# Short convolution of a hybrid backbone: own PSUM tile for the second sum of a pair, right-hand sums first, modulation later, output operands split block by block

## The chip, the cores and the metric

The kernel runs on one core of a Trainium2 chip. The metric is the device time of one execution in microseconds (us), as a median over runs. Before the change the three timed runs gave 1486.51, 1482.36 and 1488.16 us.

## What is computed

Four layers run one after the other over 640 tokens (512 latent, 128 context), each `x <- LayerNorm(alpha * x + gate * Mixer(x * (1 + scale) + shift))`, with shift, scale and gate from a modulation product of the condition vector. All is fp32. The change is in layer 1, the short gated convolution:

```
bg, cg, v, g = split(h @ w_in, 4)                  # h: 640 x 1024, w_in: 1024 x 4096
z = depthwise_conv3(cg * v) + conv_b
y = (silu(g) * bg * z) @ w_out                     # w_out: 1024 x 1024
```

## The kernel before, in words

**Products.** Each fp32 operand is kept as a high and a low part (`xh`, `xl` for tokens, `wh`, `wl` for weights), and a product is three matmuls: high by high, low by high, high by low. High parts are written by ScalarE (a cast), low parts by VectorE (a subtraction).

**Layer 1 (`sconv`).** The 1024 output channels of each of the four projections are cut in eight blocks j. Block 0 is computed directly: `mpair` gives cg and v, two calls of `mtile` give bg and g. For j = 1 to 7 `spair` runs twice, first for (cg, v), then for (bg, g): 14 pairs. A pair computes two 128-channel outputs over two halves of 320 tokens by a scheme with seven block products in place of eight. Each block product is 12 matmuls of 320 columns (four blocks of 128 inputs by three), 84 in a pair. In the order of the code they are

| product | weights | tokens | sum it goes to | read afterwards by |
|---|---|---|---|---|
| a | `a` | `xh` | x | ScalarE copy p1 |
| b | `b` | `xh` | y | VectorE add (p1 + y) |
| s2 | `s2` | `t2` | x | ScalarE copy u2 |
| s1 | `s1` | `t1` | z | ScalarE copy p5 |
| s3 | `s3` | `t3` | x | ScalarE copy u3 |
| s4 | `s4` | `xh` | z | VectorE add (u2 + z) |
| d | `d` | `t4` | x | ScalarE, negated |

Sums x and z go on accumulating after a copy, so the next product into the same sum has to follow the copy. Before the change x and z are the two halves of one two-bank tile `psxz` (pool `psmm`, two tiles of two banks), y is a one-bank tile `psy` (pool `psg`, four banks, which also holds the modulation's sums `psA`, the transposes `pt` and the output projection's sums `pso`).

**Operands of the pairs.** `token_sums` makes t1 to t4 once, after block 0's `mpair`: four sums and four splits of 128x1280. `_prep_pair` makes a pair's weights from one 1 MB load `praw`: casts on ScalarE, four sums and four low parts on VectorE. Pairs are numbered by their weight load, 52 to 65. Weights are double buffered.

**Modulation (`ada_unit`).** Layer 2's modulation is 12 units in layer 1, let in by a credit that grows with each weight taken (`rate` 0.45, twice that for a pair). A unit loads two 512 KB tiles `araw`, multiplies into `psA` and adds the result to `arows` on VectorE (L353).

**Output projection (`outproj`).** It first splits the mixer's output `o` into `xh`, `xl`, five token tiles of 128x1024 in turn. Then for the first 256 output columns it computes `pso` for the five token tiles (24 matmuls of 256 columns each), and VectorE folds each into the residual `z`. `z`, the affine vectors and the gate are loaded when the layer's buffers come free.

**Order.** A scheduler decides the order of instructions on each engine from its own estimates; `high_priority()` lets a block go ahead of others that are ready. An engine then executes its own list strictly in that order.

Of the kernel before, what the change touches and what calls it, by code (L numbers as in the profile page):

```python
# [9 lines left out]
F32 = mybir.dt.float32  # L10
# [3 lines left out]
ALU = mybir.AluOpType  # L14
AX = mybir.AxisListType

P = 128
D = 1024
KT = D // P
TS_ = 512  # L20
TP = 128
T = TS_ + TP
HALF = T // 2
SPL = (slice(0, 384), slice(384, T))
NT = T // P
# [25 lines left out]
class Kernel:  # L51
# [147 lines left out]
    def spair(self, pool, n):  # L199


        nc = self.nc
        w = self.next_w()
        N1, N2 = slice(HALF, T), slice(0, HALF)
        lo, hi = slice(0, 4), slice(4, KT)
        t = self.tops
        xz = self.psmm.tile([P, 2, 512], F32, name="psxz", tag="mm")
        y = self.psg.tile([P, 512], F32, name="psy", tag="g")
        x, z, y = xz[:, 0, :HALF], xz[:, 1, :HALF], y[:, :HALF]

        def prod(ps, wk, b, first):
            (ah, al), (bh, bl) = w[wk], b
            for k in range(4):
                for u, v, st, en in ((ah, bh, True, False), (ah, bl, False, False), (al, bh, False, True)):
                    nc.tensor.matmul(ps, lhsT=u[:, k, :], rhs=v[:, k, :], start=(first and st and k == 0),  # L215
                                     stop=(en and k == 3), skip_group_check=True)

        def keep(ps, nm, tag=None):
            o = pool.tile([P, HALF], F32, name=nm, tag=tag or nm)
            with self.tc.high_priority():  # L220
                nc.scalar.copy(out=o, in_=ps)
            return o
        oa = pool.tile([P, T], F32, name=f"ca{n}", tag=f"ca{n}")
        ob = pool.tile([P, T], F32, name=f"cb{n}", tag="cb")
        prod(x, "a", [v[:, lo, N1] for v in (self.xh, self.xl)], True)
        p1 = keep(x, "p1")
        prod(y, "b", [v[:, hi, N1] for v in (self.xh, self.xl)], True)
        prod(x, "s2", t[2], False)
        u2 = keep(x, "u2")
        with self.tc.high_priority():  # L230
            nc.vector.tensor_tensor(out=oa[:, N1], in0=p1, in1=y, op=ALU.add)
        prod(z, "s1", t[1], True)
        p5 = keep(z, "p5")
        prod(x, "s3", t[3], False)
        u3 = keep(x, "u3", "p1")
        prod(z, "s4", [v[:, hi, N2] for v in (self.xh, self.xl)], False)
        with self.tc.high_priority():
            nc.vector.scalar_tensor_tensor(out=ob[:, N2], in0=u3, scalar=-1.0, in1=p5, op0=ALU.mult, op1=ALU.subtract)
            nc.vector.tensor_tensor(out=oa[:, N2], in0=u2, in1=z, op=ALU.add)
        prod(x, "d", t[4], False)  # L240
        with self.tc.high_priority():
            nc.scalar.mul(out=ob[:, N1], in_=x, mul=-1.0)
        return oa, ob
# [87 lines left out]
    def ada_unit(self, l, c, u):  # L331


        nc = self.nc
        if u == 0 and c == (2 if l == 0 else 0):
            rows = self.adap.tile([P, 768], F32, name=f"arows{l}", tag="arows")
            nc.gpsimd.memset(rows, 0.0)
            self.arows = rows
        rows, cs = self.arows, slice(c * 256, (c + 1) * 256)
        if u == 0 and c == 2:  # L340
            ab = self.I["ada_b"][l]
            for s in range(2):
                for j in range(4):
                    o = 2 * D + j * 256
                    nc.sync.dma_start(out=rows[32 * j + s:32 * j + s + 1, cs], in_=ab[o:o + 256].unsqueeze(0))
        ps = self.psg.tile([P, 256], F32, name=f"psA{l}_{c}_{u}", tag="g")
        for k in (2 * u, 2 * u + 1):
            raw = self.rawp.tile([P, 1024], F32, name=f"araw{l}_{c}_{k}", tag="wraw")
            nc.sync.dma_start(out=raw, in_=self.I["ada_rest"][l, c, k])
            for j in range(4):  # L350
                nc.tensor.matmul(ps[32 * j:32 * j + 32, :], lhsT=self.csil[:, k, :], rhs=raw[:, j * 256:(j + 1) * 256],  # L351
                                 start=(k == 2 * u), stop=(k == 2 * u + 1), skip_group_check=True)
        nc.vector.tensor_tensor(out=rows[:, cs], in0=ps, in1=rows[:, cs], op=ALU.add)  # L353
        if u < 3:
            return
        if c == 2:
            gd = self.gate_dram[l]
            for s in range(2):
                for j in range(4):
                    nc.sync.dma_start(out=gd[s:s + 1, j * 256:(j + 1) * 256], in_=rows[32 * j + s:32 * j + s + 1, cs])  # L360
            return
        self.adafin.append(lambda: self.ada_cols(l, c, rows))
# [56 lines left out]
    def outproj(self, l):  # L419
        nc, tc = self.nc, self.tc  # L420
        last = l == self.NL - 1
        oh, ol, o, z = self.xh, self.xl, self.o, self.z
        for i in (2, 3, 4, 0, 1) if last else range(NT):
            tok = slice(i * P, (i + 1) * P)
            self.split(oh[:, :, tok], ol[:, :, tok], o[:, :, tok])
        ctx = ExitStack()
# [37 lines left out]
        def final():  # L464
            pend()
            ctx.close()
        self.pend = final

    def norm_tile(self, l, i, s, stats, tp, last):
        nc, z = self.nc, self.z  # L470
# [425 lines left out]
    def sconv(self):  # L896
        nc, tc = self.nc, self.tc
        with ExitStack() as ctx:
            sp = ctx.enter_context(tc.tile_pool(name="sp", bufs=1))
            for j in range(KT):  # L900
                if j == 0:
                    cg = sp.tile([P, T], F32, name="ca0", tag="ca0")
                    p = cg
                    pss = self.mpair()
                    for hf in range(2):
                        c = SPL[hf]
                        nc.scalar.copy(out=cg[:, c], in_=pss[hf][:, 0])
                        nc.vector.tensor_tensor(out=p[:, c], in0=cg[:, c], in1=pss[hf][:, 1], op=ALU.mult)
                    self.zctx.close()
                    tp = ctx.enter_context(tc.tile_pool(name="tp", bufs=1))  # L910
                    self.sw = ctx.enter_context(tc.tile_pool(name="sw", bufs=2))
                    self.token_sums(tp)
                else:
                    p, v = self.spair(sp, 0)
                    nc.vector.tensor_tensor(out=p, in0=p, in1=v, op=ALU.mult)
                zz = sp.tile([P, T], F32, name="zz", tag="zz")

                def cw(i):
                    return self.v("sc_conv_w", i * KT + j, 1)
                nc.scalar.activation(out=zz, in_=p, func=AF.Identity, scale=cw(1), bias=self.v("sc_conv_b", j, 1))  # L920
                self.taps(zz, p, (-1, 1), (cw(0), cw(2)))
                th = sp.tile([P, T], F32, name="th", tag="th")
                if j == 0:
                    bg = sp.tile([P, T], F32, name="ca1", tag="ca1")
                    g = sp.tile([P, T], F32, name="cb0", tag="cb")
                    ps = self.mtile()
                    nc.vector.tensor_tensor(out=self.hv(bg), in0=self.hv(zz), in1=ps, op=ALU.mult)
                    ps = self.mtile()
                    nc.scalar.activation(out=self.hv(th), in_=ps, func=AF.Tanh, scale=0.5)
                    nc.vector.scalar_tensor_tensor(out=self.hv(g), in0=self.hv(th), scalar=1.0, in1=ps, op0=ALU.add,  # L930
                                                   op1=ALU.mult)
                    nc.vector.scalar_tensor_tensor(out=self.o[:, j, :], in0=g, scalar=0.5, in1=bg, op0=ALU.mult,
                                                   op1=ALU.mult)
                    continue
                bg, g = self.spair(sp, 1)
                for c in (slice(0, HALF), slice(HALF, T)) if j == KT - 1 else (slice(0, T),):
                    nc.vector.tensor_tensor(out=bg[:, c], in0=zz[:, c], in1=bg[:, c], op=ALU.mult)
                    nc.scalar.activation(out=th[:, c], in_=g[:, c], func=AF.Tanh, scale=0.5)
                    nc.vector.scalar_tensor_tensor(out=g[:, c], in0=th[:, c], scalar=1.0, in1=g[:, c], op0=ALU.add,
                                                   op1=ALU.mult)  # L940
                    nc.vector.scalar_tensor_tensor(out=self.o[:, j, c], in0=g[:, c], scalar=0.5, in1=bg[:, c],
                                                   op0=ALU.mult, op1=ALU.mult)
            self.sw = None


# [718 lines left out]
```

## Time and profile before

| | |
|---|---|
| runs | 1486.51, 1482.36, 1488.16 us (median 1486.51) |
| profiled execution | 1491.0 us, span 1489.2 us, mean granted TensorE clock 0.988 |
| TensorE matmul busy | 1432.5 us, 96% of the span |
| VectorE busy | 1084.1 us, 73% |
| ScalarE busy | 752.1 us, 51% |
| chain that ended last | PE 71%, DVE 14%, ACT 8% |

Matmuls are pipelined: a 320-column matmul shows 0.31 us of busy time, but the next one starts 0.147 us later. So busy time hides gaps, and starts are compared instead. Layer 1 goes from about 509 us (first product of `mpair`) to 749.9 us (first matmul of `outproj`).

### The profile page before, as it was taken

The page shows a single profiled execution, that of the slowest core. Times are in us where ns is not written, and L with a number is a line of the kernel's source. Part 1 is how long each engine was busy: PE and PEld are TensorE (multiplying, and loading weights), DVE is VectorE, ACT ScalarE, POOL GpSimd, SP SyncE. Part 2 cuts the span into 40 slices and gives each one's busy share as a digit, 9 for nine tenths or more (in the row PEclk, how much of TensorE's full clock was granted, in tenths as well). Part 3 has the DMA queues.
Part 4 walks back from the last instruction along what each step waited for, and adds up shares of the span by engine and source line. Part 5 has one row for each costly group of instructions (what it writes and reads, how often), then busy time and mean ns, then how long its engine had stood idle before and what let it go on. Part 6 is the DMA issues. An engine that isn't in the chain of part 4 may idle for free.

```text
span 1489.2 us, 26175 instructions
## 1 busy us (share of the span) xinstructions
PE 1432.5 (96%) x10570; PEld 1302.7 (87%) x10570; DVE 1084.1 (73%) x1987; ACT 752.1 (51%) x1350; POOL 91.8 (6%) x194
## 2 busy tenths in 40 slices
PE   6999999999999989999999999999999999999997
PEld 4889989999989889898887999899899988888796
DVE  4777577577567786877687799787746878677767
ACT  2656366346443644544435577633643367666630
POOL 0000000000000100000001011120110200000002
PEclk8999999999999999999999999999999999999999
DMA  9322324223335352434152344343123200001041
GB/s 344 113 79 99 96 68 173 78 87 105 107 105 193 139 187 86 145 116 165 44 198 90 123 142 156 136 155 112 48 77 104 78 19 17 24 25 34 29 142 71
DMA packets 48920, 160.48 MB, mean 108 GB/s; under 512 B 5840, under 2 KB 11040, under 8 KB 47008
## 3 DMA queue, kind: packets, MB, share of 16 engines
q1 hardware_dynamic: 48800, 158.82, 31.1%
q8 instruction: 83, 1.36, 0.4%
q14 instruction: 37, 0.30, 0.1%
HBM read 149.69 MB, written 9.10 MB: 107 GB/s over the span
## 4 chain that ended last, share of the span: by engine, by line
PE 71%; DVE 14%; ACT 8%; issue 3%; DMA 2%; POOL 1%; SPq 0%; POOLq 0%; DVEq 0%; ACTq 0%
PE psmm L195 14%; PE psxz L215 10%; PE pso L175 4%; PE pso L177 4%; PE pso L176 4%; PE poa L1413 3%; PE psmm L1044 2%; DVE wl L82 2%; PE ptp L1400 2%; PE psA L351 2%; PE psy L215 2%; PE psS L175 1%; PE psS L177 1%; PE psS L176 1%; PE psmm L176 1%
## 5 line engine op out<-in xcount | busy, mean ns | idle before, releaser
L195 PE MATMUL psmm<-xh,wh 128*128 128x320 f32 x784 | 187.0, 317 | 2.6 <-ACT vt L703 1.7
L80 ACT CAST wh<-wraw 128x1024 fp32r<-128x1024 f32 (+4 forms) x129 | 127.2, 997 | 119.9 <-PE pso L177 51.7
L195 PE MATMUL psmm<-xh,wl 128*128 128x320 f32 x784 | 182.2, 312 | 0.0
L195 PE MATMUL psmm<-xl,wh 128*128 128x320 f32 x784 | 181.6, 313 | 0.0
L82 DVE TENSOR_TENSOR wl<-wraw,wh 128x1024 fp32r<-128x1024 f32 (+4 forms) x129 | 147.9, 1159 | 27.5 <-ACT wh L80 27.3
L175 PE MATMUL pso<-wh,xh 128*128 128x256 f32 (+1 forms) x464 | 149.6, 323 | 1.6 <-ACT xh L163 1.1
L177 PE MATMUL pso<-wh,xl 128*128 128x256 f32 (+1 forms) x464 | 148.5, 321 | 0.8 <-DVE xl L166 0.8
L176 PE MATMUL pso<-wl,xh 128*128 128x256 f32 (+1 forms) x464 | 148.6, 321 | 0.3 <-DVE wl L82 0.3
L195 PEld LDWEIGHTS psmm<-xh,wh 128*128 128x128 f32 x784 | 131.4, 189 | 10.8 <-issue 3.5
L195 PEld LDWEIGHTS psmm<-xl,wh 128*128 128x128 f32 x784 | 131.8, 189 | 2.6 <-issue 2.4
L195 PEld LDWEIGHTS psmm<-xh,wl 128*128 128x128 f32 x784 | 132.6, 189 | 0.9 <-issue 0.8
L175 PEld LDWEIGHTS pso<-wh,xh 128*128 128x128 f32 x464 | 87.1, 188 | 9.5 <-ACT xh L163 2.2
L177 PEld LDWEIGHTS pso<-wh,xl 128*128 128x128 f32 x464 | 87.3, 188 | 8.3 <-DVE xl L166 1.0
L176 PEld LDWEIGHTS pso<-wl,xh 128*128 128x128 f32 x464 | 87.4, 188 | 7.1 <-DVE wl L82 0.5
L1384 ACT ACTIVATE pe<-psS,mx 128x768 f32<-128x768 f32 (+1 forms) x80 | 63.7, 797 | 38.8 <-DVE mx L1382 38.4
L1382 DVE TENSOR_REDUCE mx<-psS 128x1 f32<-128x768 f32 (+1 forms) x80 | 65.2, 817 | 7.8 <-PE psS L177 7.1
L1400 PE MATMUL ptp<-ident,pe 128*128 128x128 f32 x400 | 56.8, 273 | 0.8 <-ACT pe L1384 0.8
L351 PE MATMUL psA<-araw,csil 128*32 128x256 f32 x640 | 51.2, 386 | 2.8 <-DMA araw<-in_ada_rest 2.8
L447 DVE TENSOR_TENSOR t<-pso,gateb 128x256 f32<-128x256 f32 (+1 forms) x58 | 29.3, 511 | 29.6 <-PE pso L177 28.2
L177 PE MATMUL psmm<-xh,wl 128*128 128x384 f32 (+1 forms) x160 | 49.3, 308 | 1.1 <-DVE wl L82 1.1
L175 PE MATMUL psmm<-xh,wh 128*128 128x384 f32 (+1 forms) x160 | 49.8, 311 | 0.0
L176 PE MATMUL psmm<-xl,wh 128*128 128x384 f32 (+1 forms) x160 | 49.8, 311 | 0.0
(490 smaller groups left out, 3806.2 us busy)
## 6 DMA issues: line engine op xcount, KB each, us to landing
wraw<-in_wpack SPq DMA_DIRECT2D x109, 512.0 KB
araw<-in_ada_rest SPq DMA_DIRECT2D x80, 512.0 KB
praw<-in_wpack SPq DMA_DIRECT2D x14, 1024.0 KB
araw<-in_ada_first SPq DMA_DIRECT2D x16, 512.0 KB
zdram<-z SPq DMA_DIRECT2D x10, 512.0 KB
z<-zdram SPq DMA_DIRECT2D x10, 512.0 KB
gateb<-gate_dram SPq DMA_DIRECT2D x8, 512.0 KB
wraw<-in_wpack SPq DMA_DIRECT2D x8, 320.0 KB
```

What stands on the lines that cost most here:

```text
L80: self.tc.keep_in_program_order(nc.scalar.copy(out=wh[:, :n], in_=raw[:, :n]))
L82: nc.vector.tensor_tensor(out=wl[:, :n], in0=raw[:, :n], in1=wh[:, :n].bitcast(F32), op=ALU.subtract)
L175: nc.tensor.matmul(ps, lhsT=ah, rhs=bh, start=(i == 0), stop=False)
L176: nc.tensor.matmul(ps, lhsT=ah, rhs=bl, start=False, stop=False)
L177: nc.tensor.matmul(ps, lhsT=al, rhs=bh, start=False, stop=(i == n - 1))
L195: nc.tensor.matmul(ps[hf][:, :HALF], lhsT=w[:, k, :], rhs=x[:, k, hf * HALF:(hf + 1) * HALF], start=(first and k == 0), stop=(last and k = ...
L215: nc.tensor.matmul(ps, lhsT=u[:, k, :], rhs=v[:, k, :], start=(first and st and k == 0), stop=(en and k == 3), skip_group_check=True)
L351: nc.tensor.matmul(ps[32 * j:32 * j + 32, :], lhsT=self.csil[:, k, :], rhs=raw[:, j * 256:(j + 1) * 256], start=(k == 2 * u), stop=(k == 2 ...
L1382: nc.vector.reduce_max(out=mx, in_=ps[:, :nk], axis=AX.X, negate=True)
L1384: nc.scalar.activation(out=pe[:, :nk], in_=ps[:, :nk], func=AF.Exp, bias=mx[:, 0:1], accum_out=g["sm"][:, n, hp:hp + 1])
L1400: nc.tensor.transpose(pt[:, kk, :], pe[:, (k0 + kk) * P:(k0 + kk + 1) * P], self.ident)
L1413: nc.tensor.matmul(po[hp * 64:(hp + 1) * 64, 0, :nq], lhsT=v4[:, kt, vc + hp * 64:vc + (hp + 1) * 64], rhs=g["pt"][hp][:, kk, :nq], start= ...
```

## The change

The second sum z gets its own one-bank tile from `psg`; the two-bank tile then holds x alone. `token_sums` and the modulation's add on VectorE get priority. The credit rate is 0 in block 0, so that no unit is let in before the first pair. In the last block the splits of `o` for `outproj` stand among the pair's own steps, in blocks by channels and token halves, and `outproj` of layer 1 no longer splits.

```diff
-        xz = self.psmm.tile([P, 2, 512], F32, name="psxz", tag="mm")
-        y = self.psg.tile([P, 512], F32, name="psy", tag="g")
-        x, z, y = xz[:, 0, :HALF], xz[:, 1, :HALF], y[:, :HALF]
+        x = self.psmm.tile([P, 2, 512], F32, name="psx", tag="mm")[:, 0, :HALF]
+        y, z = (self.psg.tile([P, 512], F32, name=f"ps{v}", tag="g")[:, :HALF] for v in "yz")
...
-        nc.vector.tensor_tensor(out=rows[:, cs], in0=ps, in1=rows[:, cs], op=ALU.add)
+        with self.tc.high_priority():
+            nc.vector.tensor_tensor(out=rows[:, cs], in0=ps, in1=rows[:, cs], op=ALU.add)
...
-        for i in (2, 3, 4, 0, 1) if last else range(NT):
+        for i in (2, 3, 4, 0, 1) if last else () if l == 1 else range(NT):
...
+    def split_o(self, ks, tok):
+
+        self.split(self.xh[:, ks, tok], self.xl[:, ks, tok], self.o[:, ks, tok])
...
+                self.rate = 0.0 if j == 0 else 0.45
...
-                    self.token_sums(tp)
+                    with tc.high_priority():
+                        self.token_sums(tp)
...
+                if j == KT - 1:
+                    self.split_o(slice(0, 4), slice(0, HALF))
                 bg, g = self.spair(sp, 1)
+                if j == KT - 1:
+                    self.split_o(slice(4, 7), slice(0, HALF))
...
+                    if j == KT - 1:
+                        self.split_o(slice(7, 8), c)
+                        if c.start == 0:
+                            self.split_o(slice(0, 7), slice(HALF, T))
```

**The pairs, on TensorE.** Before, in the middle of the layer, around products s1 (`t1`) and s3 (`t3`) of one pair; `wh_6750` belongs to the next pair's product a:

```order
L215 MATMUL psxz<-t2h,wl_6610 128x320
L351 MATMUL psA_1_2_6877<-araw_1_4_6878,csil 32x256 x4
L351 MATMUL psA_1_2_6877<-araw_1_5_6884,csil 32x256
L215 MATMUL psxz<-t1h,wsh_6607 128x320
...
L351 MATMUL psA_1_2_6877<-araw_1_5_6884,csil 32x256 x3
L215 MATMUL psxz<-xh,wh_6750 128x320
...
L215 MATMUL psxz<-t3h,wsh_6607 128x320
```

After, the same products and the same unit:

```order
L214 MATMUL psx<-t2h,wl_6748 128x320
L214 MATMUL psz<-t1h,wsh_6745 128x320
...
L214 MATMUL psx<-t3h,wsh_6745 128x320
...
L214 MATMUL psx<-t4h,wdl_6744 128x320
L350 MATMUL psA_1_2_7017<-araw_1_4_7018,csil 32x256 x4
L350 MATMUL psA_1_2_7017<-araw_1_5_7024,csil 32x256 x4
L214 MATMUL psx<-xh,wh_6885 128x320
```

A unit stood in two parts inside the pair, with parts of the next pair's products in the other seams. It now stands whole between pairs, and from the third pair on the seven products follow one another in the code's order.

**The first pairs, on TensorE and ScalarE.** Before, TensorE finishes block 0 (`psmm`), then goes on with a unit, product b of pair 52 (`wh_5889`), a unit and product b of pair 53 (`wh_6030`); three units have been run by then:

```order
L195 MATMUL psmm<-xh,wl_5706 128x320 x2
L351 MATMUL psA_0_1_6014<-araw_0_2_6015,csil 32x256 x4
L351 MATMUL psA_0_1_6014<-araw_0_3_6021,csil 32x256 x4
L215 MATMUL psy<-xh,wh_5889 128x320
...
L351 MATMUL psA_0_2_6161<-araw_0_4_6162,csil 32x256 x4
L351 MATMUL psA_0_2_6161<-araw_0_5_6168,csil 32x256 x4
L215 MATMUL psy<-xh,wh_6030 128x320
```

After, this stands behind block 0's first `mtile` (`wl_5700`), and the second `mtile` (`wh_5705`) behind it. `wh_6000` is pair 53's, the other weights of z and the first y are pair 52's:

```order
L195 MATMUL psmm<-xh,wl_5700 128x320 x2
L214 MATMUL psy<-xh,wh_5873 128x320
...
L214 MATMUL psz<-t1l,wsh_5877 128x320
L350 MATMUL psA_0_0_6134<-araw_0_0_6135,csil 32x256 x4
L350 MATMUL psA_0_0_6134<-araw_0_1_6141,csil 32x256 x4
L214 MATMUL psy<-xh,wh_6000 128x320
...
L214 MATMUL psz<-t1h,wsl_5878 128x320
...
L195 MATMUL psmm<-xh,wh_5705 128x320 x2
```

ScalarE before makes pair 53's weights (`wh53`) ahead of the last token sum's high part `t4h`:

```order
L102 CAST wh52_5895<-praw52_5887 128x512
L102 CAST wh53_6030<-praw53_6028 128x512 x2
L102 CAST wh53_6036<-praw53_6028 128x512
L929 ACTIVATE th_5868<-psmm_5962 128x640
L102 CAST wh53_6036<-praw53_6028 128x512
L163 CAST t4h_5848<-o_104 128x1280
```

and after behind it:

```order
L102 CAST wsh53_6004<-praw53_5998 128x512
L163 CAST t4h_5848<-o_104 128x1280
L102 CAST wh52_5879<-praw52_5871 128x512
L102 CAST wh53_6000<-praw53_5998 128x512 x2
L102 CAST wh52_5879<-praw52_5871 128x512
L220 COPY p5_6081<-psz_6025 128x320
```

The token sums have moved ahead of the weights on VectorE in the same way: before, the sum for t4 (L262) follows the eight weight sums (L108) and five 128x1024 low parts; after, four weight sums and one.

**The output projection, on VectorE.** Before, in the seam to `outproj`, the splits (L166) follow the last block's steps:

```order
L941 SCALAR_TENSOR_TENSOR o_104<-cb1_7912,ca1_7911 128x320
L166 TENSOR_TENSOR xl_103<-o_104,xh_102 128x8x128 x2
L939 SCALAR_TENSOR_TENSOR cb1_7912<-th_7902,cb1_7912 128x320
L941 SCALAR_TENSOR_TENSOR o_104<-cb1_7912,ca1_7911 128x320
L166 TENSOR_TENSOR xl_103<-o_104,xh_102 128x8x128 x3
L82 TENSOR_TENSOR wl67_8063<-wraw67_8061,wh67_8062 128x1024
```

After, most of them stand inside the last pair (a further one, 128x4x320, three blocks earlier):

```order
L166 TENSOR_TENSOR xl_103<-o_104,xh_102 128x7x320
L237 SCALAR_TENSOR_TENSOR cb1_7928<-u3_7996,p5_7982 128x320
...
L166 TENSOR_TENSOR xl_103<-o_104,xh_102 128x3x320
...
L166 TENSOR_TENSOR xl_103<-o_104,xh_102 128x320
L951 SCALAR_TENSOR_TENSOR o_104<-cb1_7928,ca1_7927 128x320
L166 TENSOR_TENSOR xl_103<-o_104,xh_102 128x320
L82 TENSOR_TENSOR wl67_8077<-wraw67_8075,wh67_8076 128x1024
```

Behind the last step of the mixer there remains one split of 128x320 in place of three of 128x1024.

## Rows read from the trace of the kernel before

**Rows 1.** Windows of 10 us, all engines: busy time (count), clock, DMA share, GB/s.

```profile
550.00:560.00 10.00, 10.00 (x54) 9.62 (x53) 3.19 (x6) 2.31 (x5) 0.00 (x0) 0.78 0.24 97
...
740.00:750.00 10.00, 8.19 (x49) 7.13 (x50) 4.85 (x10) 2.56 (x5) 0.00 (x0) 1.00 0.17 52
```

**Rows 2.** Windows of TensorE, L215 alone (x is the number of pair matmuls).

```profile
569.54:712.28 142.74, 131.51 (x841) 1.00 0.40 133
712.28:749.86 37.58, 34.18 (x216) 1.00 0.13 43
```

**Rows 3.** Windows of TensorE, L351 alone (modulation, 16 records a unit).

```profile
569.54:712.28 142.74, 13.46 (x127) 1.00 0.40 133
```

**Rows 4.** Timeline of TensorE in a middle pair: start, busy us, instruction, [wait].

```profile
596.20 1.05 PE L351 MATMUL psA<-araw,csil 128*32 128x256 f32 x10
597.18 0.42 PE L215 MATMUL psxz<-t1h,wsh 128*128 128x320 f32 x1
597.44 0.31 PE L215 MATMUL psxz<-t1l,wsh 128*128 128x320 f32 x1
...
598.91 0.31 PE L215 MATMUL psxz<-t1h,wsl 128*128 128x320 f32 x1
```

**Rows 5.** Timeline of TensorE in the last pair.

```profile
738.54 0.31 PE L215 MATMUL psxz<-t2h,wl 128*128 128x320 f32 x1
739.95 0.42 PE L215 MATMUL psxz<-t1h,wsh 128*128 128x320 f32 x1 [1.09 <-ACT u L221]
...
747.68 0.41 PE L215 MATMUL psxz<-t4h,wdh 128*128 128x320 f32 x1 [0.58 <-DVE ca L239]
```

**Rows 6.** Timeline of TensorE around the first pairs.

```profile
518.94 0.62 PE L351 MATMUL psA<-araw,csil 128*32 128x256 f32 x2
...
525.17 1.06 PE L351 MATMUL psA<-araw,csil 128*32 128x256 f32 x14
526.16 0.56 PE L195 MATMUL psmm<-xh,wh 128*128 128x320 f32 x2
...
540.45 1.07 PE L351 MATMUL psA<-araw,csil 128*32 128x256 f32 x16
...
548.76 0.60 PE L215 MATMUL psy<-xh,wh 128*128 128x320 f32 x1 [2.58 <-DVE arows L353]
549.17 0.47 PE L215 MATMUL psy<-xl,wh 128*128 128x320 f32 x1
549.43 0.47 PE L215 MATMUL psy<-xh,wl 128*128 128x320 f32 x1
```

**Rows 7.** Timeline of VectorE there.

```profile
530.86 3.10 DVE L108 TENSOR_TENSOR praw<-praw 128x512 f32<-128x512 f32 x5
...
536.14 2.35 DVE L105 TENSOR_TENSOR wl<-praw,wh 128x1024 fp32r<-128x1024 f32 x2
...
542.42 1.48 DVE L262 SCALAR_TENSOR_TENSOR o<-o 128x1280 f32<-128x1280 f32 x1
...
549.27 0.81 DVE L930 SCALAR_TENSOR_TENSOR cb<-th,psmm 128x640 f32<-128x640 f32 x1
```

**Rows 8.** Timeline of ScalarE, first pairs.

```profile
543.93 1.26 ACT L163 CAST t4h<-o 128x1280 fp32r<-128x1280 f32 x1 [0.78 <-DVE o L262]
553.72 0.62 ACT L102 CAST wh<-praw 128x512 fp32r<-128x512 f32 x1 [8.52 <-PE psxz L215]
554.24 0.42 ACT L221 COPY p<-psxz 128x320 f32<-128x320 f32 x1
```

**Rows 9.** Timeline of TensorE, start of the output projection.

```profile
749.86 0.39 PE L175 MATMUL pso<-wh,xh 128*128 128x256 f32 x1 [0.16 <-ACT xh L163]
...
765.12 0.39 PE L175 MATMUL pso<-wh,xh 128*128 128x256 f32 x1 [0.49 <-DVE t L447]
```

**Rows 10.** Timeline of VectorE, start of the output projection.

```profile
761.29 1.76 DVE L451 TENSOR_TENSOR z<-z,lng 128x256 f32<-128x256 f32 x5
...
764.65 0.75 DVE L447 TENSOR_TENSOR t<-pso,gateb 128x256 f32<-128x256 f32 x2
```

## The prediction

> **What bounds the kernel now.** The page's shares come first: TensorE is busy 96% of the span and holds 71% of the chain that ended last. So a change can gain only where TensorE stands still or runs slowly, and 96% says little, since a pipelined matmul shows twice its real spacing. The next view is therefore TensorE's timeline in layer 1, where starts are compared. In a stretch without a gap ten 320-column matmuls follow in 1.47 us, 0.147 us each [rows 4]; a unit of 16 modulation records takes 1.0 us (its row shows 1.07 with the tail) [rows 6]. With these two prices the windows give the loss by stretch.
>
> In the ten pairs from 569.54 to 712.28 us there are 841 pair matmuls and 127 modulation records [rows 2, 3]: 841 x 0.147 + 7.9 units x 1.0 = 131.5 of 142.7 us, so **11.2 us** are lost, 1.1 a pair. From 712.28 to 749.86 us, 216 matmuls [rows 2] make 31.8 and a few records 0.4 of 37.6 us: **5.4 us** lost. In the middle pairs the loss sits at the seams: ten records that should take 0.63 us are followed by the next product only 0.98 us after their start, and that product's first matmul takes 0.26 us [rows 4]. In the last pair there is no unit left to fill the seams and the waits show: 1.26 us before s1, which waits for the copy u2 of the *other* sum, and 2.4 us over the next three products (7.73 us for 36 matmuls) [rows 5].
>
> The timelines of VectorE and ScalarE around the first pairs show a third loss. TensorE waits 2.58 us for VectorE to free a modulation bank, and resumes at half speed: 0.26 us a matmul [rows 6], and the granted clock of the ten us from 550 on is 0.78 [rows 1]. As the clock has two levels, 1.2 and 2.4 GHz, that mean puts the return to full speed at about 554.4 us. The fourth loss is the start of the output projection: the fifth token tile starts 15.26 us after the first [rows 9], while 96 matmuls of 256 columns need 96 x 0.118 = 11.3 us (0.118 is 0.147 scaled by columns, an estimate): **4.0 us** lost.
>
> **The change part by part.** *Own tile for z, middle pairs.* Products and units stay the same in number. What goes is the wait of s1 for u2 and the second seam of each unit. With x, z, x, z in the order of the list, each product that follows a copy has another product of 12 x 0.147 = 1.76 us between. The round trip to be covered is the last matmul's 0.31 us [rows 4] and the copy's 0.42 us [rows 8], 0.73 us. If ScalarE is free there is 1.0 us to spare and the wait is nothing. If two casts (0.62 us each [rows 8]) stand in front of every copy, 0.73 + 1.24 - 1.76 = 0.2 us is left at each of three copies, 0.6 a pair. I take 0.2 a pair, near the first end, as ScalarE is about half busy. A whole unit's seam costs about 0.2 us: 14 records take 0.99 us to the next start [rows 6] where 0.88 is their work, and the first matmul behind them takes 0.1 more. Eight units and ten pairs leave 1.6 + 2.0 = 3.6 of 11.2 us: **7.6 us** gained, between 3.6 and 9.6.
>
> The Trainium skill ("PSUM — Partial Sum Buffer", section "PSUM bank collisions raise a hardware error") says that two engines must be kept apart by bank and quadrant. The old halves of `psxz` were already two banks, so by that rule s1 need not have waited for the copy of x, an own tile brings nothing, and the sum would shrink to the 3.3 us of the first pairs and the projection. The trace disagrees that no wait stood there: 1.09 us, released by ScalarE's copy u.
>
> *Last stretch.* The same cause, plus a unit that the later credit leaves for these pairs. Of 5.4 us some 0.7 stay (two pairs at 0.2, a seam, the hand-over): **4.7 us**, between 3 and 5.4.
>
> *Split operands.* The splits' elements are the same; all but one small block move under the last pair, whose VectorE and ScalarE have room (4.85 and 2.56 us busy of 10) [rows 1]. The first four token tiles then run nearly without waits. The fifth needs a bank that VectorE frees at L447 (764.65 us now), behind the affine steps that start at 761.29 us [rows 10], and those need the residual, affine and gate loads, which start only when the last pair's buffers are free, as before. If the gate landed just before 764.65 us the gain is 0.5 us; if the loads are never late it is 4.0. VectorE's affine steps stand in the row without a wait, so it was VectorE that was late; I take **2.8 us**.
>
> *Priority of the token sums, no units in block 0.* Here a new wait comes. TensorE loses 16 records ahead of the first `mtile` (1.6 us and seams [rows 6]), which then starts at about 524.4 in place of 526.16 us and ends 48 x 0.147 us later, at 531.4. Product b of pair 52, two matmuls and a unit bring it to 534.7 us; next in its list is pair 53's b, which needs `wh53`. On ScalarE that cast now stands behind `t4h`, and `t4h` behind the t4 sum on VectorE. That sum started at 542.42 us; four weight sums (0.62 each), four low parts (1.18 each) and a short add (about 0.4) no longer stand ahead of it [rows 7], so it starts at 542.4 - 7.6 = 534.8 and ends at 536.3. With `t4h` (1.26) and three casts (0.62) [rows 8] `wh53` is there at 539.4 us: TensorE stands for 4.7 us. Then two weight sums, a modulation add (0.4), t4's low part (1.48) and the four low parts, 8.2 us with the add that frees the bank of the second `mtile`, reach 544.5 us. TensorE has 28 products to run meanwhile. At full clock the second `mtile` ends at 551.9 us; if the clock is halved for as long after the wait as now (548.76 to 554.4, 5.6 us), at 553.7.
>
> At that point 45 pair matmuls and one unit are done. Before, it was 18 and three at about 550.4 us, when x's first product starts (VectorE's read of the second `mtile`, which frees its bank, ends at 550.1 us [rows 7]). To come level, before needs 27 x 0.147 = 4.0 us more and the half clock's 15 x 0.12 = 1.8, and is owed two units, 2.4: 553.8 us. So the head gains 0.1 to 1.9 us, less some 0.5 for p1, which now stands behind a cast in the first pairs: **0.5 us**. Its bounds are -4 (the half clock lasts through the second `mtile`, 2 us, and the weights land as much later) and +3 (no half clock, VectorE a step earlier).
>
> *Priority of the modulation's add.* 0.4 us on VectorE moves; nothing waits for it but the bank of the unit. Nothing.
>
> **Sum.** 0.5 + 7.6 + 4.7 + 2.8 = 15.6 us, against the profiled execution's 1491.0: 1475.4 us. That execution lies 4.5 us above the median of the runs shown (1486.51), so the prediction is **1471 us**. Layers 2 and 3 keep their order and are TensorE's; the gain is carried to the end.
>
> **The rivals.**
> 1. *ScalarE's list holds the copies up.* Casts wait for weight sums and stand in front of copies. For: an engine's list is strict, and one cast that waits stops the copy behind it. Against: 1.0 us to spare at each copy. At the upper price (0.6 a pair, twelve pairs) and with one more late cast a pair, 6 us are lost again: gain 9 to 10, 1477.
> 2. *The first pairs get worse.* The 4.7 us wait is longer than any now, and the half clock follows it. At the bound the head costs 4 us: gain 11, 1475.5; with a load late too, 1478.
> 3. *The change doesn't do what it says in the pairs*: the seams stay, since the unit's filling hid the wait already and the remaining 1.1 us a pair is something else. For: in the middle pairs the row names no wait. Then only the last pair's 3.7 us and part of the projection are gained, 4 to 6: 1481.
> 4. *Slower: the clock falls in the pairs.* Without the filling each product stands against its copy's wait; if the short idle pieces make the clock fall, a pair at 1.2 GHz takes 84 x 0.12 = 10.1 us more. It decides from 2.3 pairs at half clock on (15.6 + 7.4 = 23 us, 1494 us); three pairs give 1486.5 - 15.6 + 30.3 = 1501 us. Against: in the last pair, with a wait at almost every product, the clock stayed 1.00 [rows 1]. The Trainium skill ("TensorE: Matmul & The Clock Gate", section "A second HAM failure mode: psum-queue depth-cycling") describes a kernel in which such short idles between groups made the clock swing; no row here shows it.
>
> **How the numbers follow.** Forecast 0.60 (gain 12 to 19, 1467.5 to 1474.5 us by itself), rival 1 0.16, rival 2 0.09, rival 3 0.10, rival 4 0.05. 0.5% of 1486.5 is 7.4 us, about what a measurement here can tell from no change. Faster by more: the forecast, rival 1 and two thirds of rival 2, 0.82; within: rival 3 and the rest, 0.13; slower: 0.05. The range runs from 1465 (head and pairs at their better bounds, gain 21) to 1480 us (rivals 1 and 2 in it, rival 3 out).
>
> **What would show it.** Own tile: in the middle pairs no wait of s1 for u, t1-to-t1 distance 13.5 us with a unit in place of 14.5. Last pair: 12.4 us with no bracket over 0.3. Head: one wait of about 5 us near 535 us, released by ScalarE's `wh`, and a half clock after it. Projection: fifth tile 12 to 13 us after the first. It would be wrong if copies appear as releasers in every pair, if the clock is below 1.00 after 560 us, or if later layers take the gain back.

## The result and the profile after

The changed kernel takes **1474.6 us** (median of four runs, 1473.4 to 1475.7) against 1485.8 us (four runs, 1482.4 to 1488.2): ratio 0.993, 95% interval 0.990 to 0.995. The forecast was 1471 us within 1465 to 1480. The profiled execution has a span of 1472.1 us in place of 1489.2, so 17.1 us less. Of these, 2.15 lie ahead of layer 1, whose first product starts at 507.29 us in place of 509.44. From there to the projection's first matmul it is 224.97 in place of 240.42 us: 15.45 gained. From there to the last of the 240 projection matmuls of 256 columns it is 33.80 in place of 32.28 us: 1.5 lost. What follows gains 1.1. So 13.9 us lie in the places that were changed, and 3.2 outside of them, where both executions do the same work. There the granted clock differs, 0.94 against 1.00 from 300 to 360 us (the kernel before first, then the changed one; behind the busy time: granted clock, DMA share, GB/s) and 0.96 against 1.00 from 920 to 960 us:

```profile
300.00:360.00 60.00, 56.09 (x445) 0.94 0.31 104
300.00:360.00 60.00, 56.09 (x470) 1.00 0.34 113
```

**The pairs.** The windows over pairs 54 to 63 and over the last two, pair matmuls first, modulation records behind, answer [rows 2, 3]. Each row gives busy time and count of TensorE's matmuls, then of its weight loads.

```profile
571.87:706.32 134.45, 125.85 (x841) 123.27 (x841) 1.00 0.42 145
706.32:732.26 25.94, 25.01 (x168) 24.65 (x168) 1.00 0.33 103
```

```profile
571.87:706.32 134.45, 9.64 (x147) 3.76 (x144) 1.00 0.42 145
706.32:732.26 25.94, 1.14 (x20) 0.42 (x16) 1.00 0.33 103
```

The counts include records that only reach into the window; the ten pairs are 840 matmuls, and 144 weight loads are 9 whole units. With the forecast's two prices, 840 x 0.147 and 9 units x 1.0 us make 132.5 of 134.45 us: 2.0 us lost. Counted in the same way, the kernel before loses 11.4 us (840 matmuls and 126 records start in its window): 9.4 us gained. In the last two pairs 0.2 us of the loss is left, the seam of their one unit. TensorE's timeline shows a seam, which answers [rows 4], and the last pair, which answers [rows 5].

```profile
597.67 0.31 PE L214 MATMUL psx<-t4h,wdl 128*128 128x320 f32 x1
597.91 1.07 PE L350 MATMUL psA<-araw,csil 128*32 128x256 f32 x16
598.91 0.41 PE L214 MATMUL psx<-xh,wh 128*128 128x320 f32 x1
599.16 0.31 PE L214 MATMUL psx<-xl,wh 128*128 128x320 f32 x1
...
719.84 0.41 PE L214 MATMUL psx<-xh,wh 128*128 128x320 f32 x1
...
732.12 0.31 PE L214 MATMUL psx<-t4h,wdl 128*128 128x320 f32 x1
732.26 0.28 PE L175 MATMUL pso<-wh,xh 128*128 128x256 f32 x1
```

A whole unit now stands in one place, where before it was cut up to fill waits: 1.0 us of work, and 0.24 and 0.25 us in place of 0.147 for the steps at its two ends. The last pair takes 732.26 - 719.84 = 12.42 us without one wait in brackets. Before, besides the two waits of [rows 5], it had these two; each of the four is released by the read of the *other* sum of the pair (u is a copy of x, p here a copy of z, and ca reads z):

```profile
742.49 0.41 PE L215 MATMUL psxz<-t3h,wsh 128*128 128x320 f32 x1 [0.52 <-ACT p L221]
745.07 0.42 PE L215 MATMUL psxz<-xh,wh 128*128 128x320 f32 x1 [0.56 <-ACT u L221]
```

**The first pairs.** TensorE there, in answer to [rows 6]:

```profile
531.97 1.07 PE L350 MATMUL psA<-araw,csil 128*32 128x256 f32 x16
536.80 0.63 PE L214 MATMUL psy<-xh,wh 128*128 128x320 f32 x1 [3.77 <-ACT wh L102]
537.23 0.47 PE L214 MATMUL psy<-xl,wh 128*128 128x320 f32 x1
...
542.72 0.36 PE L214 MATMUL psz<-xh,wh 128*128 128x320 f32 x1
...
551.27 0.31 PE L214 MATMUL psx<-xh,wh 128*128 128x320 f32 x1
```

TensorE waits once, 3.77 us, for `wh`, then runs at half speed (1.2 GHz) for 5.9 us. What is late can be read on VectorE and then on ScalarE: the t4 sum, `t4h`, and only behind it the casts of the next pair's weights (in answer to [rows 7, 8]).

```profile
532.41 1.49 DVE L261 SCALAR_TENSOR_TENSOR o<-o 128x1280 f32<-128x1280 f32 x1
```

```profile
533.93 1.26 ACT L163 CAST t4h<-o 128x1280 fp32r<-128x1280 f32 x1 [2.18 <-DVE o L261]
535.10 2.17 ACT L102 CAST wh<-praw 128x512 fp32r<-128x512 f32 x4
```

The windows answer [rows 1] (the last columns are granted clock, DMA share and GB/s):

```profile
530.00:540.00 10.00, 6.23 (x41) 5.20 (x41) 10.00 (x11) 5.09 (x8) 0.00 (x0) 0.80 0.31 105
540.00:550.00 10.00, 10.00 (x61) 10.00 (x61) 5.67 (x10) 1.35 (x2) 0.00 (x0) 0.86 0.33 107
550.00:560.00 10.00, 10.00 (x66) 9.45 (x66) 5.22 (x7) 4.07 (x8) 0.00 (x0) 1.00 0.32 105
...
734.00:744.00 10.00, 9.89 (x83) 9.66 (x81) 5.68 (x9) 3.31 (x4) 0.00 (x0) 1.00 1.01 374
744.00:748.00 4.00, 0.72 (x4) 0.51 (x4) 3.54 (x11) 0.00 (x0) 0.00 (x0) 0.95 1.02 417
748.00:752.00 4.00, 4.00 (x25) 4.00 (x24) 4.00 (x13) 1.05 (x1) 0.00 (x0) 0.62 0.52 207
```

**The start of the projection.** TensorE, VectorE and the DMA queue of SyncE; the first two answer [rows 9, 10].

```profile
743.95 0.28 PE L177 MATMUL pso<-wh,xl 128*128 128x256 f32 x1
747.51 0.51 PE L175 MATMUL pso<-wh,xh 128*128 128x256 f32 x1 [3.28 <-DVE t L447]
```

```profile
736.30 3.50 DVE L82 TENSOR_TENSOR wl<-wraw,wh 128x1024 fp32r<-128x1024 f32 x3 [0.46 <-ACT wh L80]
743.13 1.77 DVE L451 TENSOR_TENSOR z<-z,lng 128x256 f32<-128x256 f32 x5 [3.33 <-DMA lng<-in_ln_g]
745.36 1.77 DVE L451 TENSOR_TENSOR z<-z,lnb 128x256 f32<-128x256 f32 x5 [0.46 <-DMA lnb<-in_ln_b]
747.04 0.75 DVE L447 TENSOR_TENSOR t<-pso,gateb 128x256 f32<-128x256 f32 x2
```

```profile
732.50 2.26 SPq L1532 DMA_DIRECT2D z<-zdram  x5
734.81 0.45 SPq L403 DMA_DIRECT2D lng<-in_ln_g  x1
735.30 0.45 SPq L405 DMA_DIRECT2D lnb<-in_ln_b  x1
735.86 0.87 SPq L395 DMA_DIRECT2D gateb<-gate_dram  x2
```

In the kernel before, the queue issues these loads from 749.73 us on:

```profile
749.73 2.29 SPq L1518 DMA_DIRECT2D z<-zdram  x5
```

The first four token tiles no longer wait, and the fifth still starts 15.25 us after the first (15.26 before). All pieces of its wait are now one piece of 3.28 us. VectorE is ready for the affine steps 3.33 us before the loads are, while the DMA share stands at 1.0. And behind the long wait the clock falls, which it did not do here before: 0.62 in the window from 748 us.

### The profile page after: what moved, and what is told of

The parts are those of the page before. It is cut to its first block, busy times and chain, and to the rows that moved or that the text cites. A ratio compares the mean times of both kernels' runs of the same rounds, so it can differ in the third digit from the quotient of the medians.

```text
span 1472.1 us, 26193 instructions
## 1 busy us (share of the span) xinstructions
PE 1416.0 (96%) x10570; PEld 1299.0 (88%) x10570; DVE 1085.2 (74%) x1987; ACT 751.0 (51%) x1350; POOL 86.0 (6%) x194
## 4 chain that ended last, share of the span: by engine, by line
PE 71%; DVE 14%; ACT 8%; DMA 3%; issue 3%; POOL 1%; SPq 0%; POOLq 0%; DVEq 0%; ACTq 0%
PE psmm L195 14%; PE psx L214 7%; PE pso L175 4%; PE pso L177 4%; PE pso L176 4%; PE psz L214 3%; PE poa L1427 3%; PE psmm L1058 2%; DVE wl L82 2%; PE ptp L1414 2%; PE psA L350 2%; PE psy L214 2%; DVE tr L1088 1%; PE psS L175 1%; PE psS L177 1%
## 5 line engine op out<-in xcount | busy, mean ns | idle before, releaser
L447 DVE TENSOR_TENSOR t<-pso,gateb 128x256 f32<-128x256 f32 (+1 forms) x58 | 29.2, 510 | 31.3 <-PE pso L177 30.1
L1427 PE MATMUL poa<-pT,v 128*64 128x256 f32 (+1 forms) x416 | 48.8, 377 | 0.7 <-ACT pT L1416 0.4
```

The lines of the kernel that those rows point to most:

```text
L1427: nc.tensor.matmul(po[hp * 64:(hp + 1) * 64, 0, :nq], lhsT=v4[:, kt, vc + hp * 64:vc + (hp + 1) * 64], rhs=g["pt"][hp][:, kk, :nq], start= ...
```

## The experiments

The theory after this reading: the own tile carries the gain; the block-wise split brings nothing since the nine loads (512 KB each) release the fifth token tile; the first pairs come out even. The rivals stand with each run. All twelve kernels were timed against the kernel before on the same chip. The last two columns are intervals in each profiled execution, in us. "Head edits" are the two edits of the first pairs, the credit and the priority of the token sums. In layer 1 of the kernel before, the credit's rate is 0.4 (0.45 is layer 0's); the change sets it to 0 in block 0 and to 0.45 behind it, so "undone" means 0.4 throughout.

| kernel | time, us | ratio (95%) | layer 1's first product to projection | projection, 240 matmuls |
|---|---|---|---|---|
| before, first profile | 1485.8 | | 240.42 | 32.28 |
| before, again | 1487.3 | 1.001 (0.999-1.003) | 237.96 | 32.77 |
| changed | 1474.6 | 0.993 (0.990-0.995) | 224.97 | 33.80 |
| tile alone | 1470.1 | 0.989 (0.988-0.991) | 220.85 | 31.43 |
| changed, no tile | 1493.6 | 1.005 (1.003-1.007) | mixed | mixed |
| changed, old splits | 1471.5 | 0.991 (0.989-0.993) | 226.21 | 31.51 |
| changed, loads by columns | 1469.2 | 0.989 (0.987-0.991) | 224.09 | 28.72 |
| changed, both head edits undone | 1469.0 | 0.988 (0.986-0.989) | 218.39 | 35.21 |
| changed, credit undone | 1471.1 | 0.990 (0.988-0.991) | 220.35 | 34.32 |
| changed, sums' priority undone | 1469.8 | 0.989 (0.987-0.990) | 218.25 | 33.95 |
| changed, t4 late | 1471.9 | 0.990 (0.988-0.992) | 220.39 | 36.64 |
| changed, add's priority undone | 1473.3 | 0.991 (0.989-0.993) | 222.75 | 34.87 |
| tile alone, loads by columns | 1471.9 | 0.989 (0.987-0.991) | 220.99 | 32.50 |
| both head edits undone, loads by columns | **1463.3** | 0.984 (0.983-0.986) | 218.52 | 28.73 |

**Tile alone**: the first five lines of the diff in "The change", on the kernel before.

> The kernel before with one edit: z gets its own PSUM tile. Theory (the tile carries nearly the whole gain): middle pairs 13.5 us with a unit and 12.6 without, the last pair 12.4 us, the first pairs and the projection as in the kernel before; from layer 1's first product to the first output-projection product 226 to 228 us where the kernel before has 240.4 and the changed one 225.0, and 1473 to 1476 us. Rival (the later, higher rate of modulation units or the earlier token sums make the pairs run through): the pairs stay near 14 us, 1480 us or more.

Measured: 1470.1 us, below the changed kernel, and 220.85 us, lower than expected. The pairs take 13.5 us with a unit and 12.56 without, and the rest is at the first pairs, which I had expected unchanged. There two brackets of 0.52 and 0.51 us are left, and the clock stays at 1.00:

```profile
530.00:540.00 10.00, 10.00 (x80) 1.00 0.31 105
540.00:550.00 10.00, 8.97 (x69) 1.00 0.73 247
```

So the theory was incomplete: the tile mends the first pairs too, and the other edits together take 4.5 us back (by the medians; the two intervals touch at 0.990 to 0.991). At the projection TensorE waits 1.17 and 0.76 us, and the clock falls behind these short waits:

```profile
730.00:734.00 4.00, 3.72 (x19) 0.60 0.98 389
```

The edit also moves z to the pool with four banks. No run keeps x and z as two tiles of one pool, so tile and pool are not separated; the releasers in the last pair of the kernel before, reads of the other half, speak for the tile.

**Changed, no tile** (the same five lines the other way round, in the changed kernel).

> The changed kernel with only z's own tile undone. Theory: the gain of the pairs goes, 237 to 240 us from layer 1's first product to the projection's first, 1484 to 1488 us. Rival (the other edits carry a part of it): under 235 us, 1481 or less.

Measured: 1493.6 us, above what either expected, and slower than before by 0.3 to 0.7%. The pairs are back at about 14.5 us with a unit. The first pairs have two long waits:

```profile
538.95 0.64 PE L215 MATMUL psy<-xh,wh 128*128 128x320 f32 x1 [4.52 <-ACT wh L102]
...
544.53 0.63 PE L215 MATMUL psy<-xh,wl 128*128 128x320 f32 x1 [2.81 <-DVE wl L105]
```

Projection matmuls fill the last pair's waits here, so the two intervals mix. The tile is worth 16 us on the old kernel (1486.3 to 1470.1) and 19 us among the other edits; those alone are a loss (1493.6 against 1486.3).

**Changed, old splits**: the block-wise `split_o` calls out, the old loop over token tiles in.

```diff
-        for i in (2, 3, 4, 0, 1) if last else () if l == 1 else range(NT):
+        for i in (2, 3, 4, 0, 1) if last else range(NT):
...
```

> The changed kernel with the output operands split as before, token tile by token tile after the last pair. Theory (the residual, affine and gate loads release the fifth token tile, so the block-wise split gains nothing): the fifth tile still starts 15.0 to 15.5 us after the first, and the time is that of the changed kernel within 1.5 us, perhaps 1 us better, if TensorE's idle time stays in pieces and the clock does not fall. Rival (the split gains its 2 to 3 us and something else took them): fifth tile 17 us or more after the first, 1476.5 to 1478 us.

Measured: the fifth tile starts 14.51 us after the first, half a microsecond earlier than expected, no half clock follows, and the 240 matmuls take 31.51 us, 2.3 less than with the new splits. The last pair's first product stands 13.72 in place of 12.42 us before the projection. The net is 1.0 us for the old splits in the profile. The median is 3.1 us lower, more than the 1.5 expected, but the timed ratios overlap. The rival falls. That the clock stays at 1.00 may be luck: TensorE waits 1.12 and 0.76 us here, much as in the tile alone, whose clock fell. It did not matter there: its fifth tile, too, starts after 14.51 us. VectorE shows the cover: it works through the splits and weights while the loads arrive, and meets them without a wait.

```profile
740.17 3.49 DVE L82 TENSOR_TENSOR wl<-wraw,wh 128x1024 fp32r<-128x1024 f32 x3
743.57 1.09 DVE L451 TENSOR_TENSOR z<-z,lng 128x256 f32<-128x256 f32 x3
```

**Changed, loads by columns**: the same bytes in another order.

```diff
+            for c in (slice(0, 256), slice(256, 512), slice(512, D)):
+                for i in range(NT):
+                    nc.sync.dma_start(out=self.z[:, i, c], in_=self.zdram[i][:, c])
+                nc.sync.dma_start(out=self.lng[:, c], in_=I["ln_g"][0][c].partition_broadcast(P))
...
```

> The changed kernel with the loads behind the last pair (residual, gain, bias, gate) cut by columns: columns 0 to 255 of all of them first, then 256 to 511, then the rest; bytes the same. Theory (the loads hold VectorE, and VectorE the fourth bank): the fifth tile starts 11.3 to 12.5 us after the first, no half clock there, 3.5 to 5.5 us less than the changed kernel, 1469 to 1471 us. Rival (VectorE's own work is what is late): 14.5 us or more, the time of the changed kernel.

Measured: the fifth tile starts 11.80 us after the first, the clock stays at 1.00, the 240 matmuls take 28.72 us, 5.1 less, and the median is 5.4 us lower. The theory holds. What follows the 240 takes 0.9 us longer than in the changed kernel (706.95 against 706.01), so a part is paid back later. VectorE goes straight on from the weights to the first `t`:

```profile
734.14 3.50 DVE L82 TENSOR_TENSOR wl<-wraw,wh 128x1024 fp32r<-128x1024 f32 x3 [0.46 <-ACT wh L80]
737.55 0.41 DVE L457 TENSOR_TENSOR t<-pso,gateb 128x256 f32<-128x256 f32 x1
```

VectorE's list changed with the loads (the first `t` now stands ahead of the affine steps), so the edit is not the loads alone. But in the changed kernel L447 would, without its two waits for loads, have come at 747.04 - 3.33 - 0.46 = 743.25 us, before the fourth tile's last matmul starts (743.95). The loads were what held the fifth tile.

**The first pairs, edit by edit**, four kernels from the changed one:

```diff
-                self.rate = 0.0 if j == 0 else 0.45
...
-                    with tc.high_priority():
-                        self.token_sums(tp)
+                    self.token_sums(tp)
```

Both lines undone: 

> The changed kernel without the two edits of the first pairs: the token sums at their old priority, the credit of the modulation units 0.4 in all of layer 1. Theory (own tile alone mends the first pairs; these two edits put in the wait of 3.8 us and the half clock): no wait over 1 us and no half clock there, 219 to 221 us from layer 1's first product to the projection's first, in place of 225.0; 1468 to 1471 us. Rival (the faster kernel with the tile alone owes it to something else, such as its old splits): 224 to 226 us, 1473 to 1476 us.

The first line alone: 

> The changed kernel with the credit alone undone (0.4 in all of layer 1), the token sums early. Theory (the early t4h on ScalarE makes the wait, the missing units only bare it): the wait is still there, shorter by the two units' work, 1.5 to 2.5 us, half clock behind it; 1 to 3 us under the changed kernel, 1472 to 1474 us. Rival (the missing units make the wait): no wait over 0.5 us, 1468 to 1471 us.

The second alone: 

> The changed kernel with the token sums at their old priority, the credit still 0 in the first block. Theory (the early t4h makes the wait): no wait over 1 us at the first pairs, 219 to 222 us from layer 1's first product to the projection's first, 1468 to 1471 us. Rival (the missing units make it): wait of 2 us or more, half clock, 1473 to 1476 us.

The second for the t4 sum and its split only, t1 to t3 kept early: 

> The changed kernel with the last token sum alone (t4: its sum and its split) at the old priority; t1 to t3 stay early. Theory (the chain t4 sum on VectorE, t4h on ScalarE in front of the next pair's weight casts is the wait): 1.49 and 1.26 us leave that chain, so the wait of 3.8 us shrinks to about 1.0 us, and the half clock goes or is shorter; 221 to 223 us from layer 1's first product to the projection's first, 1469 to 1472 us. Rival (all four early sums delay the weights together, t4 is a small part): wait of 2.5 us or more, 1473 us or more.

Measured, against the 224.97 us of the changed kernel: 218.39, 220.35, 218.25 and 220.39. The old priority alone brings 6.7 us, and then the credit does not matter (0.1). With the early sums kept, the two units that the old credit puts there fill much of the wait: brackets of 0.33 and 0.94 us are left, and 4.6 us come back. That is less wait than the theory's 1.5 to 2.5 us, without its half clock, and 1471.1 us is below the theory's 1472 and just above the rival's 1471. So it takes both edits: the early sums cause the wait, and the missing units leave it bare. With t4 alone late, 1.78 us of the wait are left (1.0 expected), no half clock, and 4.6 us come back: most of the loss hangs on the chain t4 sum, `t4h`, weight casts. TensorE in that last kernel, and the windows with the old priority:

```profile
536.18 0.42 PE L214 MATMUL psz<-t1h,wsl 128*128 128x320 f32 x1 [1.78 <-DVE wsl L105]
```

```profile
530.00:540.00 10.00, 10.00 (x70) 1.00 0.21 67
540.00:550.00 10.00, 10.00 (x78) 1.00 0.53 188
```

With both undone the layer comes out just under the 219 to 221 us of the theory, the time inside its bounds. In all four the projection is no faster (33.95 to 36.64 us in place of 33.80): TensorE still comes to the late loads, and a part of what the layer gains is lost there. Both undone: 6.6 us less in the layer, 5.6 in the median.

**Add's priority undone** (the `with` ahead of the modulation's add out). 

> The changed kernel with the high priority of the modulation's add undone. Theory (nothing waits for that add): the time of the changed kernel within 1.5 us, 1473 to 1476 us, the wait at the first pairs the same 3.8 us, perhaps 0.4 shorter. Rival (the add in front delays the weights): wait of 3.0 us or less, 1471 us or less.

Measured: 1473.3 us, inside the theory's bounds, but 222.75 us in the layer. The wait is cut in two, and the clock does not fall:

```profile
535.95 0.41 PE L214 MATMUL psz<-t1h,wsl 128*128 128x320 f32 x1 [2.80 <-DVE wsl L105]
...
540.22 0.41 PE L214 MATMUL psz<-xh,wl 128*128 128x320 f32 x1 [1.47 <-DVE wl L105]
```

The first wait meets the rival's sign (3.0 us or less), the time doesn't (1471 or less). 4.3 us of waits cost less here than 3.8 and a half clock; the projection then takes 1.1 us more. The timed ratios overlap, so the edit is worth about nothing in the end, but not for the reason given.

**Tile alone, loads by columns** (both edits on the kernel before). 

> The kernel before with z's own tile and the loads behind the last pair cut by columns, nothing else: operands split tile by tile after the last pair, old priorities, old credit. It tells what the block-wise split is worth once the loads come in time. Theory (it was held back by the loads alone): here the first tiles wait for their operands again, last pair to first projection product 13.7 us in place of 12.3, the fifth tile 14 to 14.6 us after the first in place of 11.8; 3 to 4.5 us more than the kernel with the block-wise split and the same loads (1463.3), 1466 to 1468 us. Rival (the split brings nothing either way): 1462 to 1464.5 us.

Measured: 1471.9 us, above the 1466 to 1468 expected, and the fifth tile 15.58 us after the first, outside of 14 to 14.6. Last pair to projection 13.67 in place of 12.33 us and 32.50 in place of 28.73 for the 240 matmuls: with the loads in time the block-wise split is worth 5.1 us, above the 3 to 4.5 expected. Some of the 5.1 is the clock, 0.67 here from 730 to 734 us behind waits of 1.17 and 0.76 us, where it stays at 1.00 with the early splits. The early loads without the early splits gain nothing (32.50 against 31.43 us for the tile alone); TensorE now waits a second time for a split:

```profile
737.05 0.39 PE L177 MATMUL pso<-wh,xl 128*128 128x256 f32 x1 [0.77 <-DVE xl L166]
```

**Both head edits undone, loads by columns.** 

> The changed kernel without the two edits of the first pairs, and with the loads behind the last pair cut by columns (columns 0 to 255 of all of them first). Theory: the gains of the two places add, 5.4 us at the first pairs and 5.0 at the projection, 1463 to 1466 us; projection's first product to its 240th matmul 28.7 us. Rival (one of them is lost later, in layer 2's start): 1468 us or more.

Measured: 1463.3 us (1461.4 to 1466.5), 218.52 and 28.73 us: the two gains add. This is the fastest version, 1.4 to 1.8% under the kernel before. In the profiled execution, the slowest of its four, 3.1 us come back behind the 240 matmuls (709.13 us against 706.01 in the changed kernel), about half of it soon behind them (0.9 in all with the loads by columns above) and half at a stretch of lower clock (0.96 from 920 to 960 us).

**The kernel before, again.** 

> The kernel before, unedited, profiled a second time: the first profiled execution (1491.0 us) lies 4.5 to 5 us above the median. Theory (the excess is spread: some us ahead of layer 1, some in layer 1): layer 1's first product 1 to 2 us earlier than 509.4 us and 237 to 240 us from it to the projection's first in place of 240.4. Rival (the excess lies wholly outside layer 1): 240.4 within 0.5 us again, and the gain of 15.4 us in layer 1 stands also between executions at the median.

Measured: an execution of 1487.0 us, 3.9 less than the first. Layer 1 starts 2.1 us earlier, just beyond the 1 to 2 expected, and takes 2.5 less; the rest is 0.6 longer. From pair 54 to the projection both take 177.8 us, so the 2.5 us lie in the first pairs, where TensorE's waits are shorter than in the first profile. There the 2.58 us of [rows 6] stand behind another wait, which those rows leave out:

```profile
545.55 0.64 PE L351 MATMUL psA<-araw,csil 128*32 128x256 f32 x8 [1.51 <-DMA araw<-in_ada_rest]
```

The same two waits in the second profile:

```profile
543.21 0.64 PE L351 MATMUL psA<-araw,csil 128*32 128x256 f32 x8 [1.28 <-DMA araw<-in_ada_rest]
545.12 0.38 PE L215 MATMUL psy<-xh,wh 128*128 128x320 f32 x1 [1.28 <-DVE arows L353]
```

## Why the prediction was right, and where it was not

- **Middle pairs**: 7.6 us predicted, 11.4 - 2.0 = 9.4 measured, near the upper bound. I took 0.2 us a pair for copies held up by casts; no bracket shows such a wait. Rival 1 falls, and rival 3 with it: the tile alone takes the pairs from 14.5 to 13.5 us. By the Trainium skill's rule ("PSUM — Partial Sum Buffer", section "PSUM bank collisions raise a hardware error") the two old halves, being two banks, needed no separation; the waits were there all the same, and the tile alone, 16 us faster, takes them out. So keeping banks apart was not what decided the wait.
- **Last stretch**: 4.7 predicted, 5.2 measured (5.4 lost before, 0.2 after: 25.94 us for two pairs whose work is 25.7).
- **First pairs**: 0.5 predicted; 15.45 - 9.4 - 5.2 = 0.85 is left, and the wait (3.77 us, 4.7 forecast), its releaser, its place (536.80 us; about 539.4 forecast, 2.15 us of it the earlier start of the layer) and the half clock came as worked out. (The "28 products" of that working are 28 matmuls: 28 products would take 49 us.) But the second profile of before makes it a loss of about 1.6 us against a usual execution, and the tile alone shows what the sum never asked: what the first pairs would gain by the tile without the other two edits. Undoing these gives 6.6 us. The parts were priced together, so a loss stood hidden in a gain.
- **Split operands**: the mis-sized term. 2.8 us predicted, between 0.5 and 4.0; measured 0.0 at the fifth tile and -1.5 over the 240 matmuls; against the old splits in the changed kernel the edit is worth -1.0. The failing step is "VectorE's affine steps stand in the row without a wait, so it was VectorE that was late". A row without a wait says that the loads landed no later than VectorE came, not how much earlier. By an estimate they had landed only just before. In the changed kernel VectorE's two waits for them end 10.6 and 12.9 us after the queue issues the first load (743.13 and 745.36 against 732.50). Counted from the first load of the kernel before (749.73 us) that is 760.4 and 762.6 us, and VectorE came at 761.29 [rows 10] and 762.97. So the fifth tile could gain less than 1 us. The half clock behind the one long wait, which the bounds left out, took the rest.
- **The profiled execution and the median**: the last step took the 4.5 us between them off the sum as though they lay outside the change. 2.5 us of a surplus of 3.9 lay in the first pairs, the very wait that the change replaces, so they were counted twice. The sum itself, 1475.4 us, is within 1 us of the median that was measured, and that is partly luck: the pairs gave 2.3 us more than predicted, the split 4.3 less, and 3.2 us of the difference between the two profiled executions lie where nothing was changed.
- **Rivals 2 and 4**: against the second profile of before the first pairs are worse by 1.6 us, well inside rival 2's bound of 4. Without the tile the first pairs are worse still, with two long waits, 1493.6 us in all. The clock stays 1.00 in the pairs, so rival 4 fell.

Layer 1 starts between 506.0 and 510.4 us in executions whose TensorE work is ordered alike up to there, some 4 us that no edit here touches. The clock goes with it: the four executions with 1.00 from 300 to 360 us start layer 1 at 506.0 to 507.3 us, the ten with 0.94 or 0.97 there at 507.3 to 510.4. What stays open is why the clock falls there in some executions and not in others.

## What to carry to other kernels

Price each edit of a bundle against the others done, not only against the kernel before: the one edit that gained by itself was worth 16 us, and two of its companions gave back 6.6 us in the layer. When waits in front of a transfer's user are cleared, ask how early the transfer lands, not whether it is waited for now; loading first the columns that are read first gave 5 us where the splits stood early, and nothing where they did not. An engine's strict list makes "earlier" for one cast "later" for the weights behind it.

## What the runs showed of the hardware

The clock did not follow the length of the longest wait alone. It went to its lower level during or just behind every single wait of 3.28 to 5.12 us in layer 1 and the projection of these profiles (0.62 from 748 to 752 us in the changed kernel, behind 3.28). Shorter waits went either way. In the second profile of before it fell just behind two of 1.28 us with modulation records between (0.83 in 540 to 550 us); it stayed at 1.00 behind 2.80 and 1.47 us with pair matmuls between. At the start of the projection it fell behind 1.17 and 0.76 us in the tile alone (0.60 from 730 to 734 us) and stayed at 1.00 behind 1.12 and 0.76 us with the old splits. No rule for the shorter waits comes out of these runs.

Loads cut into rows of 1 and 2 KB kept the DMA engines busy for fewer bytes: the kernel with loads by columns shows 263 GB/s at a DMA share of 0.86 while its loads run, the changed kernel, with rows of 4 KB, 374 GB/s at 1.01 from 734 to 744 us. Divided by the share that is about 306 against 370 GB/s, an estimate.

```profile
732.00:748.00 16.00, 15.89 (x134) 1.00 0.86 263
```
